# Three value chunks of the spatial gating as blocks in seven products, and its spatial weights loaded at the layer's beginning

## The chip, the core and the metric

The kernel runs on one core of one Trainium2 chip, as one program of some 29,000 instructions. The metric is device time in microseconds (us), the median of several runs.

## The reference, cut to what matters

Two stacks of two layers each work on one sequence of 512 tokens with 1024 features, all in float32. The last layer but the feed-forward is the spatial gating:

```
z = gelu(h @ w_in + b_in)                 # 512x1024 @ 1024x4096
u, v = split(z, 2)                        # 2048 features each
v = layernorm(v, ln_g, ln_b)              # over all 2048 features of a token
sv = einsum('gts,bnsgc->bntgc', ws * tril, v in chunks of 128 tokens) + bs
y = (u * sv) @ w_out                      # 512x2048 @ 2048x1024
```

There are 16 groups g of 128 features; each has its own 128x128 matrix ws over the tokens of a chunk. Ahead of each layer and behind it stand RMS norms whose scales and shifts come from a vector c times `ada_w` (the "ada" sums below).

## The kernel before, in words

Every dense product is made of three matmuls: both operands are split into a high part (float32r, a cast on ScalarE, L191) and a low part (the difference, on VectorE, L192), and `mm3` (L287 to L289) adds high by high, high by low and low by high in one PSUM bank. The layer's input stands transposed in `XH` and `XL` (128 partitions x 8 blocks k of the features x 512 tokens).

`dense` loads a weight in pieces of 256 rows and 512 columns, splits each piece and runs it against four banks. Its tiles are "w" slots of the pool `mid` (4 KB per partition); a new tile takes the slot that has been free for longest, and waits until all its readers are done. The pool `small` (2 KB per partition) has lists "c", "f" and "m" that work alike; `share` moves idle slots between lists.

`seven` computes a product of four blocks by seven block products instead of eight (Winograd's form of Strassen). The token side has `Sums`: four sums of blocks of `XH` and `XL`, each split again. The weight side loads four blocks of 512 rows and 256 columns, makes four differences on GpSimd (L411, L415, L420, L425), splits seven operands, runs seven products of 2 x 4 `mm3` with 256 columns (ring `seven_bank` of six banks) and combines them on ScalarE (L413) and VectorE (L421 to L441); `done` takes each finished block. The feed-forward uses it for six of its eight chunks, in pairs, with the features on the partitions; there `Sums` is made while a dense stage runs, and its fourth sum overwrites a block of `XH` and `XL`.

The spatial gating, `sgu`, makes the 2048 value features in four chunks of 512, with the tokens on the partitions. Chunk 0 (`by_block_first`) goes token block by token block, as the blocks of `XH` are finished. Chunks 1 to 3 go through `dense` with `by_token`. Each bank gets the bias (L1473, VectorE), gelu (L1474, ScalarE) and statistics (L1476, VectorE). Then come mean and variance, and `gate(p)` for p = 0 to 3: normalise the values of chunk p (L1509 to L1511), load 4 groups of spatial weights (`raw`, L1514), transpose them on TensorE (L1517), mask them (L1519), run the dense product of the u half, multiply the values with the spatial weights on TensorE (L1530), add, multiply with u and split. Between gate(2) and gate(3) stands the first half of the output product.

The ada sums are put in between as steps. Each step issues a load of 256 KB and one VectorE operation (L571, L573) into an accumulator; `dense` runs `ada_rate` steps per piece (`ada_go`), and `sgu` has three sums of 20 steps, of which 16 have an operation. What is left is flushed behind gate(3) (`ada_go()`).

All DMAs are issued from SP's queue. The order on each engine is made at build time from the program: among the instructions that the planner holds ready, the one written first goes first; on the chip every engine then keeps that order.

Of the kernel before, what the change touches and what calls it, by code (L numbers as in the profile page):

```python
# [10 lines left out]
F32R = mybir.dt.float32r  # L11
# [19 lines left out]
def kernel(ctx: ExitStack, tc: tile.TileContext, inp: dict, out: bass.AP):  # L31
# [7 lines left out]
    class Ring:  # L39
        def __init__(self, items):  # L40
            self.items, self.i = items, 0
# [78 lines left out]
    def blk(i):  # L120
        return slice(i * P, (i + 1) * P)
# [7 lines left out]
    def by_block(ap):  # L129
        return ap.rearrange("p (c t) -> p c t", t=P)  # L130
# [58 lines left out]
    def split(hi, lo, src):  # L189

        S.copy(hi, src)  # L191
        V.tensor_sub(lo, src, hi.bitcast(F32))  # L192
# [158 lines left out]
    class Sums:  # L351

        def __init__(self):
            def blocks(t):
                return [[t[:, 4 * h : 4 * h + 4, 256 * i : 256 * i + 256] for h in range(2)] for i in range(2)]

            h, l = blocks(XH), blocks(XL)
            hf, lf = ([[b.bitcast(F32) for b in r] for r in m] for m in (h, l))  # L360
            s = [[mid.new("a", [4, 256], F32R) for _ in range(2)] for _ in range(3)]
            s1, s2, s3 = (mid.new("w", [4, 256]) for _ in range(3))
            G.tensor_tensor(s2, lf[1][0], lf[1][1], op=add)
            V.tensor_add(s1, hf[1][0], hf[1][1])
            V.tensor_add(s1, s1, s2)
            split(*s[0], s1)
            G.tensor_tensor(s3, lf[0][0], lf[1][0], op=sub)
            V.tensor_sub(s2, s1, hf[0][0])
            V.tensor_sub(s2, s2, lf[0][0])
            split(*s[1], s2)  # L370
            V.tensor_sub(s1, hf[0][0], hf[1][0])
            V.tensor_add(s3, s3, s1)
            split(*s[2], s3)
            V.tensor_sub(s1, hf[0][1], s2)
            V.tensor_add(s1, s1, lf[0][1])
            split(h[1][0], l[1][0], s1)
            mid.free(s1, s2, s3)
            self.held = [t for p in s for t in p]
            self.of = {"11": (h[0][0], l[0][0]), "12": (h[0][1], l[0][1]), "22": (h[1][1], l[1][1])}
            self.of.update({f"s{i + 1}": s[i] for i in range(3)}, s4=(h[1][0], l[1][0]))  # L380

        def free(self):
            mid.free(*self.held)

    def seven(w, c0, c1, left, done):

# [10 lines left out]
        def product(at, right):  # L399
            b = seven_bank.next()  # L400
            for c in range(2):
                for k in range(4):
                    lh, ll = (t[:, k, blk(c)] for t in right)
                    rh, rl = (t[:, k, :] for t in left.of[at])
                    mm3(b[:, 256 * c : 256 * c + 256], lh, ll, rh, rl, k == 0, k == 3)
            mid.free(*right)
            return b
# [1046 lines left out]
    def sgu(then):  # L1454
# [5 lines left out]
        def row_in(ap):  # L1460
            t = small.new("c", [512])
            nc.sync.dma_start(t, ap.to_broadcast([P, 512]))
            return t
# [25 lines left out]
            return bank  # L1489

        values(0, by_block_first)
        mid.share(w=11, a=16)
        ada_col_steps(1, 3)
        ada_col_steps(1, 4)
        ada_sum(1, 2, lambda: None)
        ada_rate[0] = 2
        for c in range(1, 4):
            values(c, lambda c: dense(w_in, 0, KD, [(2048 + 512 * c, 512)], by_token).__getitem__)
        for tb in range(NB):
            mu, rs = mean_rstd(stats[tb], 1e-6)  # L1500
            V.tensor_copy(v_norm[:, tb, 0:1], rs)
# [2 lines left out]
        def gate(p):  # L1504
# [5 lines left out]
                V.tensor_mul(v, v, gr)  # L1510
                G.tensor_add(v, v, br)  # L1511
            small.free(gr, br)
            raw = row_c.new("c", [512])
            nc.sync.dma_start(by_block(raw), inp["b_ws_2"][0, 4 * p : 4 * p + 4].rearrange("g t s -> t g s"))  # L1514
            b = aux_bank.next()
            for c in range(4):
                T.transpose(b[:, blk(c)], raw[:, blk(c)], ident)  # L1517
# [19 lines left out]
            VV[p].free()  # L1537
            return O

        row_c = small  # L1540
        O = [gate(0), gate(1)]
        Y = [[small.new("f", [512]) for _ in range(2)] for _ in range(NB)]
        of = lambda p, tb: (lambda k: O[p + k // 4](k % 4, blk(tb)))
# [62 lines left out]
```

## Time and profile before

| | us |
|---|---|
| median of 3 runs | 2278.05 (2271.94 to 2279.82) |
| the profiled execution | 2284.42 |
| its span in the trace | 2282.7 |
| TensorE busy | 2226.5 (98%) |
| VectorE busy | 1466.1 (64%) |
| ScalarE busy | 974.4 (43%) |
| GpSimd busy | 236.2 (10%) |

Engines: PE is TensorE, PEld its weight loads, DVE VectorE, ACT ScalarE, POOL GpSimd, SP the queue that issues DMAs. Times in the trace are us from the span's start. A busy TensorE is not TensorE at its peak, since matmuls overlap; distances from start to start tell more. A row of a group reads: line, engine, operation, output <- inputs, shapes, count | busy us, mean ns | idle time ahead of it and what ended it. A wait is put down to the releaser that came last by the profile; where that engine had long been done, it was another, often a DMA.

### The profile page before, as it was taken

The numbers are of one execution on the slowest core, as the hardware profiler recorded it, in microseconds if no ns is written. First come the engines' busy times: TensorE is split into PE (matmuls) and PEld (weight loads), VectorE is DVE, ScalarE is ACT, GpSimd is POOL, SyncE is SP. The second block draws the span as 40 slices with busy tenths as digits, with TensorE's granted clock in tenths as the row PEclk, the third lists the DMA queues.
The fourth block names the chain that finished last, engine by engine and source line by source line (L and its number), as shares of the span: only waits on it lengthen the run. The fifth ranks groups of instructions, "written<-read, shape, count | busy, mean of one in ns | idle before, by whom it ended". The sixth has DMA issues, their size and how long they took to land.

```text
span 2282.7 us, 29350 instructions
## 1 busy us (share of the span) xinstructions
PE 2226.5 (98%) x11112; PEld 1829.6 (80%) x11112; DVE 1466.1 (64%) x2610; ACT 974.4 (43%) x1784; POOL 236.2 (10%) x209
## 2 busy tenths in 40 slices
PE   8999999999999999999999999999999998999998
PEld 6787788787777777887777888988777787898997
DVE  5665755844995857843547847867656747655765
ACT  4333344335344544333444534525524335443543
POOL 0000000100000000100211131221002201031130
PEclk9999999999999999999999999999999999999999
DMA  5343434222222125224413435353254543323322
GB/s 172 111 135 103 146 90 127 93 62 65 85 73 74 38 88 157 79 66 124 144 56 120 156 108 166 103 175 111 74 159 151 157 147 104 108 83 97 116 93 83
DMA packets 158062, 251.16 MB, mean 110 GB/s; under 512 B 13784, under 2 KB 59056, under 8 KB 157920
## 3 DMA queue, kind: packets, MB, share of 16 engines
q1 hardware_dynamic: 157920, 249.29, 34.8%
q8 instruction: 87, 1.43, 0.3%
q14 instruction: 55, 0.45, 0.1%
HBM read 247.15 MB, written 2.10 MB: 109 GB/s over the span
## 4 chain that ended last, share of the span: by engine, by line
PE 77%; DVE 10%; DMA 6%; issue 3%; ACT 3%; POOL 1%; SPq 0%; POOLq 0%; DVEq 0%; ACTq 0%
PE bank L287 23%; PE bank L288 23%; PE bank L289 23%; DMA small<-in_ada_w_dram 3%; DVE mid L192 3%; DVE small L573 2%; PE bank L1109 2%; PE bank L294 1%; DMA mid<-in_ffn_w_dram 1%; ACT mid L191 1%; POOL tiny_c L480 1%; PE bank L1288 1%; PE bank L1293 1%; PE bank L1124 1%; DMA mid<-in_gla_w_in_dram 0%
## 5 line engine op out<-in xcount | busy, mean ns | idle before, releaser
L192 DVE TENSOR_TENSOR mid<-mid,mid 128x512 fp32r<-128x512 f32 (+2 forms) x530 | 512.6, 988 | 457.2 <-ACT mid L191 291.3
L191 ACT CAST mid<-mid 128x512 fp32r<-128x512 f32 (+2 forms) x530 | 419.8, 818 | 769.3 <-DMA mid<-in_ffn_w_dram 139.1
L287 PE MATMUL bank<-mid,mid 128*128 128x512 f32 (+1 forms) x1320 | 491.9, 373 | 5.3 <-DVE small L441 2.7
L288 PE MATMUL bank<-mid,mid 128*128 128x512 f32 (+1 forms) x1320 | 488.3, 370 | 0.0
L289 PE MATMUL bank<-mid,mid 128*128 128x512 f32 (+1 forms) x1320 | 488.1, 370 | 0.0
L287 PE MATMUL bank<-xt_hi,mid 128*128 128x512 f32 (+1 forms) x1216 | 430.2, 355 | 14.7 <-ACT xt_hi L191 9.5
L288 PE MATMUL bank<-xt_lo,mid 128*128 128x512 f32 (+1 forms) x1216 | 428.7, 353 | 3.2 <-DVE xt_lo L192 3.2
L289 PE MATMUL bank<-xt_hi,mid 128*128 128x512 f32 (+1 forms) x1216 | 427.7, 352 | 0.0
L287 PEld LDWEIGHTS bank<-mid,mid 128*128 128x128 f32 x1320 | 248.0, 188 | 53.5 <-DVE small L441 3.5
L289 PEld LDWEIGHTS bank<-mid,mid 128*128 128x128 f32 x1320 | 248.2, 188 | 45.1
L288 PEld LDWEIGHTS bank<-mid,mid 128*128 128x128 f32 x1320 | 248.2, 188 | 43.3 <-issue 0.5
L287 PEld LDWEIGHTS bank<-xt_hi,mid 128*128 128x128 f32 x1216 | 232.5, 192 | 50.9 <-ACT xt_hi L191 11.6
L288 PEld LDWEIGHTS bank<-xt_lo,mid 128*128 128x128 f32 x1216 | 233.2, 192 | 35.6 <-DVE xt_lo L192 4.2
L289 PEld LDWEIGHTS bank<-xt_hi,mid 128*128 128x128 f32 x1216 | 232.8, 191 | 32.1 <-issue 1.3
L287 PE MATMUL bank<-mid,xt_hi 128*128 128x512 f32 (+1 forms) x640 | 252.6, 395 | 0.7 <-ACT mid L191 0.7
L289 PE MATMUL bank<-mid,xt_lo 128*128 128x512 f32 (+1 forms) x640 | 250.4, 391 | 0.8 <-DVE xt_lo L192 0.8
L288 PE MATMUL bank<-mid,xt_hi 128*128 128x512 f32 (+1 forms) x640 | 250.3, 391 | 0.4 <-DVE mid L192 0.4
L573 DVE SCALAR_TENSOR_TENSOR small<-small,c_act,small 128x512 f32<-128x512 f32 x168 | 133.5, 809 | 73.9 <-DMA small<-in_ada_w_dram 72.8
L289 PEld LDWEIGHTS bank<-mid,xt_lo 128*128 128x128 f32 x640 | 120.6, 188 | 28.2 <-DVE xt_lo L192 1.7
L287 PEld LDWEIGHTS bank<-mid,xt_hi 128*128 128x128 f32 x640 | 120.7, 189 | 26.3 <-ACT mid L191 1.2
L288 PEld LDWEIGHTS bank<-mid,xt_hi 128*128 128x128 f32 x640 | 120.6, 188 | 26.2 <-DVE mid L192 0.9
L480 POOL TENSOR_TENSOR tiny_c<-tiny_c,minus_half 128x1 f32<-128x1 f32 (+1 forms) x68 | 53.9, 794 | 722.5 <-DVE tiny_c L494 375.4
(299 smaller groups left out, 2305.4 us busy)
## 6 DMA issues: line engine op xcount, KB each, us to landing
mid<-in_ffn_w_dram SPq DMA_DIRECT2D x128, 512.0 KB, 3.7
small<-in_ada_w_dram SPq DMA_DIRECT2D x192, 256.0 KB, 2.9
mid<-in_dsa_w_in_dram SPq DMA_DIRECT2D x36, 512.0 KB, 3.5
mid<-in_gla_w_in_dram SPq DMA_DIRECT2D x32, 512.0 KB, 4.2
mid<-in_b_w_in_dram SPq DMA_DIRECT2D x32, 512.0 KB, 3.7
mid<-in_a_w_in_dram SPq DMA_DIRECT2D x24, 512.0 KB, 3.9
mid<-in_gla_w_in_dram SPq DMA_DIRECT2D x32, 256.0 KB, 3.0
mid<-in_gla_w_out_dram SPq DMA_DIRECT2D x16, 512.0 KB, 3.7
```

The lines of the kernel that those rows point to most:

```text
L191: S.copy(hi, src)
L192: V.tensor_sub(lo, src, hi.bitcast(F32))
L287: T.matmul(o, lhsT=lh, rhs=rh, start=start, stop=False)
L288: T.matmul(o, lhsT=lh, rhs=rl, start=False, stop=False)
L289: turns.passed(o, T.matmul(o, lhsT=ll, rhs=rh, start=False, stop=stop))
L294: i = T.transpose(b[:, blk(c)], src, ident)
L480: G.tensor_tensor(r, v, minus_half[:, 0:m], op=ALU.pow)
L573: V.scalar_tensor_tensor(a, t, ck, a, op0=mult, op1=add)
L1109: T.matmul(b[:, :n], lhsT=QT[tb][:, blk(c)], rhs=KT[:, :n], start=True, stop=True)
L1124: T.transpose(b[:, blk(c)], es[c][:, blk(j)], ident)
L1288: T.matmul(sb[:, :n], lhsT=KT[pr, c // 2, blk(j)], rhs=QT[pr, c // 2, j * P :], start=True, stop=True)
L1293: T.matmul(nb[i // 2][:, (i % 2) * 129 : (i % 2) * 129 + 129], lhsT=Dm[j][:, blk(i - j)], rhs=vv[j][:, c, :], start=j == 0, stop=j == i)
```

## The change

Chunks 1 to 3 of the values go through `seven` instead of `dense`. For this `Sums(True)` keeps the fourth sum in tiles of its own, since the gates still read `XH` and `XL`, and `seven` gets `by_tokens`: the blocks of tokens become the stationary operand and the blocks of the weight the moving one, so that the tokens stand on the partitions as before. `values_seven` adds the bias to a combined block, applies gelu and takes the statistics once a pair of token blocks is complete. The four loads of spatial weights are issued ahead of the sums into four tiles of list "f", and `gate` takes its own from there. List "c" has 11 tiles instead of 7 during the value chunks. `seven` runs no ada steps.

```diff
-        def __init__(self):
+        def __init__(self, keep=False):
...
-            s = [[mid.new("a", [4, 256], F32R) for _ in range(2)] for _ in range(3)]
+            s = [[mid.new("a", [4, 256], F32R) for _ in range(2)] for _ in range(4 if keep else 3)]
+            s4 = s[3] if keep else (h[1][0], l[1][0])
...
-            split(h[1][0], l[1][0], s1)
+            split(*s4, s1)
...
-            self.of.update({f"s{i + 1}": s[i] for i in range(3)}, s4=(h[1][0], l[1][0]))
+            self.of.update({f"s{i + 1}": s[i] for i in range(3)}, s4=s4)
...
-    def seven(w, c0, c1, left, done):
+    def seven(w, c0, c1, left, done, by_tokens=False):
...
-                    lh, ll = (t[:, k, blk(c)] for t in right)
-                    rh, rl = (t[:, k, :] for t in left.of[at])
+                    still, move = (left.of[at], right) if by_tokens else (right, left.of[at])
+                    lh, ll = (t[:, k, blk(c)] for t in still)
+                    rh, rl = (t[:, k, :] for t in move)
...
         values(0, by_block_first)
+        raws = [small.new("f", [512]) for _ in range(4)]
+        small.share(c=11, f=6)
         mid.share(w=11, a=16)
         ada_col_steps(1, 3)
         ada_col_steps(1, 4)
         ada_sum(1, 2, lambda: None)
         ada_rate[0] = 2
+        for p in range(4):
+            nc.sync.dma_start(by_block(raws[p]), inp["b_ws_2"][0, 4 * p : 4 * p + 4].rearrange("g t s -> t g s"))
+        sums = Sums(True)
+
+        def values_seven(c):
+            VV.append(Quad())
+            br = row_in(inp["b_b_in_2"][:, 2048 + 512 * c : 2560 + 512 * c])
+
+            def done(t, n, b):
+                at = slice(256 * n, 256 * n + 256)
+                b2 = b.rearrange("p (i e) -> p i e", e=256)
+                V.tensor_add(b2, b2, bc(br[:, at], 1, [2, 256]))
+                S.activation(VV[c].ts[t][:, :, at], b2, AF.Gelu)
+                small.free(b)
+                if t != n:
+                    for tb in (2 * t, 2 * t + 1):
+                        V.bn_stats(stats[tb][:, c, :], VV[c][tb])
+
+            c0 = 2048 + 512 * c
+            seven(w_in, c0, c0 + 256, sums, done, True)
+            small.free(br)
+
         for c in range(1, 4):
-            values(c, lambda c: dense(w_in, 0, KD, [(2048 + 512 * c, 512)], by_token).__getitem__)
+            values_seven(c)
...
-            raw = row_c.new("c", [512])
-            nc.sync.dma_start(by_block(raw), inp["b_ws_2"][0, 4 * p : 4 * p + 4].rearrange("g t s -> t g s"))
+            raw = raws[p]
...
-        row_c = small
+        sums.free()
+        small.share(c=7, f=10)
         O = [gate(0), gate(1)]
```

## Rows read from the trace of the kernel before

**Rows 1.** The page's busy times: us, share of the span, instructions of each engine.
```profile
PE 2226.5 (98%) x11112; PEld 1829.6 (80%) x11112; DVE 1466.1 (64%) x2610; ACT 974.4 (43%) x1784; POOL 236.2 (10%) x209
```
**Rows 2.** Stretches of the spatial gating: start:end, length, busy us (instructions) of each engine, granted clock of TensorE, share of the DMA engines, GB/s. Chunks 1 to 3 run from 1637.9, gate(0) to gate(2) from 1705, gate(3) from about 1840.
```profile
1640.00:1660.00 20.00, 20.00 (x88) 16.23 (x87) 8.51 (x10) 6.16 (x8) 0.00 (x0) 1.00 0.34 113
...
1700.00:1720.00 20.00, 16.55 (x68) 13.22 (x67) 15.93 (x32) 10.41 (x15) 6.29 (x10) 0.91 0.57 179
...
1740.00:1760.00 20.00, 17.00 (x74) 13.69 (x73) 14.98 (x24) 4.63 (x6) 5.13 (x4) 0.91 0.48 132
1760.00:1780.00 20.00, 18.49 (x100) 15.47 (x99) 15.17 (x24) 7.02 (x10) 0.00 (x0) 1.00 0.63 184
...
1840.00:1860.00 20.00, 20.00 (x90) 16.28 (x89) 6.64 (x6) 4.87 (x6) 0.00 (x0) 1.00 0.43 135
...
1710.00:1712.00 2.00, 2.00 (x8) 1.61 (x7) 2.00 (x6) 0.00 (x1) 0.00 (x0) 0.50 0.63 173
```
**Rows 3.** TensorE's waits, first two of the spatial gating (1590 to 1900 us), then one of the first feed-forward (1270 to 1560 us): us in total, times, longest.
```profile
PE bank L1517 <- DVE mid L1510: 4.5, 2, 3.0
PE bank L1517 <- DMA small<-in_b_ws_dram: 3.4, 1, 3.4
...
PE bank L287 <- DVE small L433: 1.7, 1, 1.7
```
**Rows 4.** TensorE's timeline at the three groups of transposes: start, us, instruction, and in brackets the idle time before it and what ended it.
```profile
1709.33 1.12 PE L1517 MATMUL bank<-ident,small 128*128 128x128 f32 x4 [3.45 <-DMA small<-in_b_ws_dram]
1710.09 0.78 PE L288 MATMUL bank<-xt_lo,mid 128*128 128x512 f32 x1
...
1712.37 0.45 PE L287 MATMUL bank<-xt_hi,mid 128*128 128x512 f32 x1
...
1746.54 1.02 PE L1517 MATMUL bank<-ident,small 128*128 128x128 f32 x4 [3.00 <-DVE mid L1510]
...
1777.86 0.63 PE L1517 MATMUL bank<-ident,small 128*128 128x128 f32 x4 [1.51 <-DVE mid L1510]
1778.24 0.48 PE L289 MATMUL bank<-xt_hi,mid 128*128 128x512 f32 x1
```
**Rows 5.** DMA issues of two tensors: count, KB each, median us from issue to landing.
```profile
mid<-in_b_w_in_dram SPq DMA_DIRECT2D x32, 512.0 KB, 3.7
...
small<-in_b_ws_dram SPq DMA_DIRECT2D x4, 256.0 KB, 2.8
```
**Rows 6.** Timeline of SP and VectorE around the end of chunk 0, and SP's issue of the spatial weights of gate(1).
```profile
1626.90 0.38 SPq L614 DMA_DIRECT2D small<-in_norm_g_dram  x1
1633.92 4.50 SPq L210 DMA_DIRECT2D mid<-in_b_w_in_dram  x3
...
1630.68 0.69 DVE L192 TENSOR_TENSOR xt_lo<-small,xt_hi 128x512 fp32r<-128x512 f32 x1
...
1638.06 0.69 DVE L1473 TENSOR_TENSOR small<-bank,small 128x512 f32<-128x512 f32 x1 [3.47 <-PE bank L289]
...
1743.60 0.37 SPq L1514 DMA_DIRECT2D small<-in_b_ws_dram  x1
```
**Rows 7.** TensorE's timeline: the first matmul of chunk 1, the last of chunk 3, the first of gate(0).
```profile
1637.86 0.39 PE L287 MATMUL bank<-mid,xt_hi 128*128 128x512 f32 x1
...
1705.26 0.39 PE L289 MATMUL bank<-mid,xt_lo 128*128 128x512 f32 x1
1705.49 0.39 PE L287 MATMUL bank<-xt_hi,mid 128*128 128x512 f32 x1
```
**Rows 8.** A stretch of the first feed-forward in which TensorE runs products of 256 columns alone (columns as in rows 2).
```profile
1355.00:1375.00 20.00, 20.00 (x171) 20.00 (x171) 16.85 (x15) 11.74 (x18) 10.68 (x4) 1.00 0.25 79
```
**Rows 9.** VectorE's timeline in the first feed-forward: two operations of the sums one behind the other, a split beside a GpSimd subtraction, two operations of 512 one behind the other.
```profile
1291.60 1.22 DVE L369 TENSOR_TENSOR mid<-mid,xt_lo 128x1024 f32<-128x1024 f32 x1
1292.73 1.22 DVE L371 TENSOR_TENSOR mid<-xt_hi 128x1024 f32<-128x1024 f32 x1
...
1365.90 2.83 DVE L192 TENSOR_TENSOR mid<-mid,mid 128x1024 fp32r<-128x1024 f32 x1
...
1563.59 0.68 DVE L433 TENSOR_TENSOR small<-small,bank 128x512 f32<-128x512 f32 x1
1564.19 1.22 DVE L192 TENSOR_TENSOR mid<-mid,mid 128x1024 fp32r<-128x1024 f32 x1
```
**Rows 10.** Groups by shape: the first four rows and the last in a pair of `seven` of the feed-forward (1322 to 1382 us, eight GpSimd subtractions), the fifth in the value chunks (1640 to 1682 us, none).
```profile
L192 DVE TENSOR_TENSOR mid<-mid,mid 128x1024 fp32r<-128x1024 f32 x17 | 25.0, 1478 | 26.5 <-PE bank L289 11.2 <-ACT mid L191 11.0 <-PE bank L288 4.2
L192 DVE TENSOR_TENSOR mid<-small,mid 128x512 fp32r<-128x512 f32 x4 | 5.5, 1385 | 0.6 <-ACT mid L191 0.6
L423 DVE TENSOR_TENSOR small<-small,bank 128x512 f32<-128x512 f32 x2 | 1.4, 688 | 0.1
...
L425 POOL TENSOR_TENSOR mid<-mid,mid 128x1024 f32<-128x1024 f32 x2 | 4.8, 2421 | 5.3 <-issue 5.3
...
L192 DVE TENSOR_TENSOR mid<-mid,mid 128x1024 fp32r<-128x1024 f32 x9 | 11.0, 1224 | 19.8 <-ACT mid L191 19.8
...
L191 ACT CAST mid<-mid 128x1024 fp32r<-128x1024 f32 x17 | 17.7, 1050 | 32.5 <-DMA mid<-in_ffn_w_dram 16.1 <-PE bank L288 9.7 <-POOL mid L411 2.5
```
**Rows 11.** Busy time of the ada steps' operation L573 on VectorE in two stretches (count in brackets), granted clock, DMA share, GB/s.
```profile
1640.00:1705.00 65.00, 5.16 (x7) 1.00 0.45 138
...
1800.00:1865.00 65.00, 0.00 (x0) 1.00 0.46 142
```

## The prediction

> **What bounds the kernel now.** I read the page's busy shares first, then TensorE's waits in the stretch of the spatial gating, then the timeline at those waits and at both ends of the value chunks. TensorE is busy for 98% of the span [rows 1], so a change pays by fewer columns on TensorE or by closing its gaps. In the gating layer the gaps are few and sharp: while value chunks 1 to 3 run there is none, in the stretches around 1710, 1750 and 1770 us it loses 3.4, 3.0 and 1.5 us, and in the first two the granted clock falls to 0.91 on the mean [rows 2]. The list of waits puts all three at L1517, the transposes of the spatial weights, one on the DMA of `b_ws`, two on VectorE's L1510 [rows 3]. L1510 has nothing to do with a transpose of `raw`. At the second gap the load was issued at 1743.60, such a load lands after 2.8 us, and the transposes began at 1746.54 [rows 4 to 6]: all three are the same late load, issued only when a "c" tile came free.
>
> **Edit 1: the loads of the spatial weights move to the layer's beginning.** Four issues on SP, 256 KB each, go ahead of the value chunks' loads. SP had nothing to issue from 1626.9 to 1633.92 [rows 6], so they delay nobody. The gain is the three gaps, 3.45 + 3.00 + 1.51 = 8.0 us [rows 4]. After the first two TensorE ran at half speed (granted 0.50, its 1.2 GHz level) for about 3 us: four transposes took 0.76 us where they took 0.38 at the third, and five matmuls 2.28 us where they need 5 x 0.232 [rows 4]. That is 0.4 + 1.1, some 1.6 us each with the second's one more slow matmul, 3.2 in all. What is late next? The first weight pieces of each dense stage had been split before its gap, so I see no second wait behind it. Edit 1: 11.2 us gained. If only the DMA-named wait were a DMA's, it would be 3.45 + 1.6.
>
> **Edit 2, TensorE's part.** Chunks 1 to 3 start on TensorE at 1637.86 and gate(0) at 1705.49 [rows 7]: 67.6 us with 3 x 96 = 288 matmuls of 512 columns, 0.23 us from start to start (66.7 at 0.2315), and some small work that is only moved. After: 3 chunks x 7 products x 2 x 4 x 3 = 504 matmuls of 256 columns. In a stretch of the feed-forward's products 171 of these fill 20 us [rows 8]; from start to start it is 0.1183, so 59.6 us. A chunk needs 19.9 instead of 22.2 us: 7.0 us gained if nothing waits. That is seven eighths by columns, a little worse by the shorter matmul.
>
> **Edit 2, the sums.** `Sums(True)` can begin when the last `xt_lo` is written, 1630.68 + 0.6 = 1631.3, and TensorE has done chunk 0 at 1638.1 [rows 6]. In the feed-forward the same sums lie under a dense stage; here nothing else is ready for TensorE. Product "11" needs no sum, but it needs its weight block loaded, cast (ScalarE) and its low part (VectorE). The "w" tiles that were free early and took the next piece now hold the sums' scratch, so `b11` takes the tile that before got its load at 1633.92: landed at about 1637.6 (3.7 us), cast by 1638.7, and then VectorE [rows 6]. There stand the sums, written earlier in the program, and of ready instructions the order takes the one written first. They are 12 VectorE operations of 128x1024, 1.13 us from start to start [rows 9], 13.6 us, and since one can nearly always run while ScalarE casts for another, I find no hole before the last cast. So the low part of `b11` comes one operation before their end: 1631.3 + 12.5 (eleven of them) + 2.4 (the four 0.6 us operations of chunk 0's last two blocks) + 1.1 (itself) + 2.2 (two GpSimd sums beside it, below) = 1649.5. TensorE waits 11.4 us, and 1.6 us more go to its clock by the price above. Bounds: 1.8 us if it slips in at once (1638.7 + 1.2), without the clock, since the gap of 1.51 us was followed by no slow stretch; 17 us if it comes last and GpSimd stops VectorE for whole instructions three times.
>
> **Edit 2, VectorE in the products.** Per chunk it had four splits and 8 operations of 512, 9.3 us. Now: 7 splits (1.13) and 7 combinations, 4 bias additions and 4 statistics, 15 x 0.60 [rows 9, 10]: 17.0 us against 19.9 of TensorE. On top come four GpSimd subtractions per chunk, 2.4 us or more each [rows 10], which hold VectorE up. How much, c per subtraction, is the open price. From below: in the feed-forward's pair of products the 17 splits of 128x1024 average 1.478 against 1.224 in the value chunks, the 4 of 128x512 1.385 against 0.69: 4.3 + 2.8 us over 8 subtractions, 0.9 [rows 10]. At its busiest, one split took 2.83 for 1.22 [rows 9]. From above: all 2.4. I take 1.1, near the mean, since here VectorE is rarely idle. VectorE then ends its last split, and TensorE its last product, at 1631.3 + 13.6 + 2.4 + 51.0 + 14c - 4.8 (the eight small operations behind the last split) + 2.8 (the product) = 1696.3 + 14c = 1711.7. TensorE by its own columns: 1638.1 + 11.4 + 1.6 + 59.6 = 1710.7. Two bounds so close don't hide in each other: I take 1713 against 1705.5 before, 7.5 us later. Then gate(0) opens on the banks of the last products, its third tile behind the combination L441, 2.8 us after its start; VectorE will be some 4 us behind: 1.5 us (0 to 4). The feed-forward's waits on such combinations show the kind, 1.7 us at L433 [rows 3].
>
> The Trainium skill, "SBUF — State Buffer", section "SBUF: two separate sides", speaks against the change: the port pair shared by VectorE and GpSimd is an exclusive lock for a whole instruction, and the loser fully blocks. The rows agree that both slow each other, but not for whole instructions on the mean. By that rule in full c would be 2.4 and the time that of the third case below; by the rows it is about 1.
>
> **Edit 2, the `ada` steps.** `seven` calls no `ada_go`, so 24 of the 60 steps leave the value chunks in the program, 7 of their operations on VectorE (5.2 us), while none ran between 1800 and 1865 [rows 11]. Late now is the third sum, whose last 12 steps, eight of them with an operation, are flushed behind gate(3). VectorE has 6.6 us of work in 20 there [rows 2], so I cost this at 0; without that cover it is eight times 0.74, 6 us. ScalarE gets 7 casts of 1.05 us per chunk for 4 [rows 10], and is far from full.
>
> **Sum.** +7.5 + 1.5 - 11.2 = -2.2 us against the profiled execution's 2284.4: 2282.2. The same 2.2 off the median of the runs, 2278.05, is 2276.
>
> **The rivals.** (a) *The forecast*: the wait at the first product and VectorE's load eat most of the gain. 0.46. Its own range is 2272 to 2284.
> (b) *Faster*: `b11` slips into an early hole in the sums, and c is 0.8 as over the feed-forward. Then TensorE ends at 1638.1 + 1.8 + 59.6 = 1699.5 and VectorE at 1696.3 + 11.2 = 1707.5; +2.0 + 0.5 - 11.2 = -8.7: 2269. With c near 0.4 it is 2263. It takes an end of the products before 1708.4 to gain 0.3%. For it: VectorE was idle for over 3 us between 1634.5 and 1638.06 before. Against: those holes are now the sums' own. 0.29.
> (c) *Slower*: GpSimd stops VectorE for nearly whole instructions. c = 1.84 moves the end to 1722 and costs 0.3%; c = 2.4 gives 1729.9, +24.4 + 1.5 - 11.2 = +14.7: 2293; half-way, 2287. For it: three chunks without a dense stage between them, where the feed-forward has two, and its pair ends with VectorE behind. Against: the mean of 0.9. 0.20.
> (d) *The early load does not do what it says*: the two waits named L1510 are VectorE's, so 3.00 + 1.51 + 1.6 stay: 2276 + 6 = 2282. Against: issue, landing time and start fit to 0.2 us. 0.05; half of it beyond the bound.
>
> About 0.3%, 6.8 us, is what a measurement of this kernel tells from no change. Faster 0.29; same 0.46 and half of (d), 0.48; slower 0.23. The range runs from (b)'s better end, 2264, to between half and full stop of (c), 2289.
>
> **What would show it.** Right: a TensorE gap of 9 to 13 us between chunk 0 and the first product, ended by VectorE's L192, with the granted clock at half behind it; products over about 60 to 63 us; no wait at L1517; gate(0) from about 1713 to 1715. Wrong if that gap is under 5 us or over 16, if TensorE waits between the products add up to more than 6 us, if the transposes still wait, or if the flushed `ada` steps hold up the last output product at L616.

## The result, and the profile after

The changed kernel took 2304.85 us (median), the kernel before 2277.24 beside it: a ratio of 1.0118, 95% interval 1.007 to 1.0166. It is slower by some 28 us, beyond the upper end of the prediction's range (2289). The profiled executions are 2302.6 us of span after and 2282.7 before.

The page's busy times of the kernel after, to be read beside [rows 1]:

```profile
PE 2225.2 (97%) x11328; PEld 1838.6 (80%) x11328; DVE 1530.1 (66%) x2652; ACT 989.0 (43%) x1800; POOL 277.7 (12%) x223
```

TensorE's busy time hardly fell, although its columns did: matmuls at half speed count as busy. VectorE has 64 us more. To see where the 20 us of span are I cut both traces at four matmuls: the first of chunk 0, the first of gate(0), the end of the last values by spatial weights, and the first of 256 columns in the feed-forward behind. These are the stages of both, and of the experiments told below (us):

| kernel | up to chunk 0 | values | gates | output product | rest | span |
|---|---|---|---|---|---|---|
| before | 1610.6 | 94.9 | 162.3 | 54.1 | 360.9 | 2282.7 |
| after | 1607.0 | 119.9 | 156.7 | 55.8 | 363.3 | 2302.6 |
| e1, early loads alone | 1601.9 | 96.1 | 159.3 | 54.2 | 361.6 | 2273.0 |
| e2, seven products alone | 1611.4 | 120.3 | 164.5 | 56.3 | 362.8 | 2315.2 |
| e3, differences on VectorE | 1610.1 | 112.6 | 159.6 | 55.6 | 362.8 | 2300.8 |
| e4, no differences | 1605.6 | 100.7 | 159.7 | 57.5 | 362.7 | 2286.1 |
| e5, chunk 1 dense | 1616.8 | 104.8 | 161.6 | 53.5 | 361.9 | 2298.6 |
| e7, more weight tiles | 1608.8 | 115.2 | 157.5 | 55.8 | 362.3 | 2299.7 |
| e8, transposes early | 1614.2 | 96.6 | 164.7 | 53.4 | 361.8 | 2290.8 |
| e9, ada steps between | 1621.4 | 125.3 | 164.7 | 53.6 | 361.6 | 2326.6 |
| e10, e5 without differences | 1605.3 | 97.0 | 157.9 | 53.7 | 362.1 | 2275.9 |
| e12, transposes a gate ahead | 1607.7 | 95.2 | 165.8 | 53.2 | 360.6 | 2282.4 |
| e13, three ada steps | 1602.5 | 96.1 | 159.0 | 54.8 | 360.7 | 2273.1 |

The first column is work that no kernel here changes, and it varies by up to 19.5 us from one execution to the next; so one profile's span says little, and the stages are compared instead. Each row is one execution; where two kernels run nearly the same code, a stage agrees to about 1 us (values of 94.9, 96.1 and 96.1 with dense chunks, of 119.9 and 120.3 by seven). From before to after: values +25.0, gates -5.6, behind them +4.1, upstream -3.6 by chance; together +19.9.

TensorE's timeline after, at the waits of the value stage (columns as in [rows 4]):

```profile
1644.74 0.58 PE L287 MATMUL bank<-mid,xt_hi 128*128 128x256 f32 x1 [10.36 <-ACT mid L191]
...
1645.69 0.58 PE L287 MATMUL bank<-mid,mid 128*128 128x256 f32 x1 [0.37 <-ACT mid L191]
...
1647.93 0.58 PE L288 MATMUL bank<-mid,xt_hi 128*128 128x256 f32 x1 [1.66 <-DVE mid L192]
...
1654.06 0.39 PE L287 MATMUL bank<-mid,xt_hi 128*128 128x256 f32 x1 [1.51 <-ACT mid L191]
...
1680.31 0.39 PE L288 MATMUL bank<-mid,mid 128*128 128x256 f32 x1 [3.03 <-DVE mid L192]
...
1687.18 0.39 PE L288 MATMUL bank<-mid,xt_hi 128*128 128x256 f32 x1 [0.85 <-DVE mid L192]
...
1700.86 0.38 PE L288 MATMUL bank<-mid,xt_hi 128*128 128x256 f32 x1 [2.05 <-DVE mid L192]
...
1706.99 0.58 PE L288 MATMUL bank<-mid,mid 128*128 128x256 f32 x1 [3.04 <-DVE mid L192]
```

The stretches of that stage (columns as in [rows 2]):

```profile
1640.00:1660.00 20.00, 11.51 (x57) 10.31 (x57) 19.96 (x14) 8.94 (x10) 7.53 (x3) 0.63 0.04 13
1660.00:1680.00 20.00, 16.82 (x136) 16.29 (x136) 17.18 (x15) 7.05 (x9) 8.37 (x3) 1.00 0.31 106
1680.00:1700.00 20.00, 17.65 (x144) 17.21 (x144) 18.44 (x21) 7.57 (x10) 5.32 (x3) 1.00 0.33 107
1700.00:1720.00 20.00, 16.10 (x112) 15.89 (x113) 20.00 (x17) 7.58 (x9) 8.48 (x3) 0.83 0.12 32
```

Where the kernel before had TensorE full and VectorE at 8 of 20 us, VectorE is now busy for 17 to 20 of 20 us, and TensorE waits for its splits and runs at half speed (granted 0.50, 1.2 GHz) behind some of the waits: 64 starts of matmuls come 0.2 us or more apart where they need 0.118, which adds up to 6.5 us. All waits from the one ahead of the first product to gate(0) are 23.5 us. With the chunks' 59.4 us at full speed (504 by 0.1178) these are 89.4 of the 92.5 us between chunk 0's last matmul and gate(0).

The waits at the transposes of the spatial weights, [rows 3], are gone. In the gates TensorE's list of waits now reads (1726 to 1880 us):

```profile
PE bank L287 <- ACT small L1575: 2.6, 1, 2.6
PE bank L289 <- DVE mid L192: 1.9, 1, 1.9
```

### The profile page after: what moved, and what is told of

It reads as the page before. It is cut to its first block, busy times and chain, and to the rows that moved or that the text cites. A ratio compares the mean times of both kernels' runs of the same rounds, so it can differ in the third digit from the quotient of the medians.

```text
span 2302.6 us, 29877 instructions
## 1 busy us (share of the span) xinstructions
PE 2225.2 (97%) x11328; PEld 1838.6 (80%) x11328; DVE 1530.1 (66%) x2652; ACT 989.0 (43%) x1800; POOL 277.7 (12%) x223
## 4 chain that ended last, share of the span: by engine, by line
PE 76%; DVE 11%; DMA 5%; issue 3%; ACT 3%; POOL 2%; SPq 0%; DVEq 0%; POOLq 0%; ACTq 0%
PE bank L287 22%; PE bank L288 22%; PE bank L289 22%; DVE mid L192 4%; DMA small<-in_ada_w_dram 3%; PE bank L1112 2%; DVE small L576 1%; PE bank L294 1%; ACT mid L191 1%; POOL tiny_c L483 1%; PE bank L1291 1%; PE bank L1296 1%; DMA mid<-in_ffn_w_dram 1%; PE bank L1127 1%; PE bank L1556 1%
## 5 line engine op out<-in xcount | busy, mean ns | idle before, releaser
L192 DVE TENSOR_TENSOR mid<-mid,mid 128x512 fp32r<-128x512 f32 (+2 forms) x543 | 545.7, 1026 | 415.4 <-ACT mid L191 238.7
L191 ACT CAST mid<-mid 128x512 fp32r<-128x512 f32 (+2 forms) x543 | 433.2, 824 | 756.8 <-PE bank L288 140.0
L287 PE MATMUL bank<-mid,mid 128*128 128x512 f32 (+1 forms) x1416 | 522.0, 369 | 10.9 <-DVE small L444 3.1
L288 PE MATMUL bank<-mid,mid 128*128 128x512 f32 (+1 forms) x1416 | 518.6, 366 | 6.7 <-DVE mid L192 6.7
L289 PE MATMUL bank<-mid,mid 128*128 128x512 f32 (+1 forms) x1416 | 517.7, 366 | 0.0
L287 PEld LDWEIGHTS bank<-mid,mid 128*128 128x128 f32 x1416 | 268.8, 190 | 60.1 <-DVE small L444 4.0
L288 PEld LDWEIGHTS bank<-mid,mid 128*128 128x128 f32 x1416 | 268.5, 190 | 51.0 <-DVE mid L192 7.5
L289 PEld LDWEIGHTS bank<-mid,mid 128*128 128x128 f32 x1416 | 269.0, 190 | 45.2
L287 PEld LDWEIGHTS bank<-xt_hi,mid 128*128 128x128 f32 x1216 | 230.5, 190 | 49.0 <-ACT xt_hi L191 11.2
L287 PE MATMUL bank<-mid,xt_hi 128*128 128x512 f32 (+2 forms) x616 | 235.9, 384 | 12.6 <-ACT mid L191 12.6
L288 PE MATMUL bank<-mid,xt_hi 128*128 128x512 f32 (+2 forms) x616 | 233.8, 379 | 5.1 <-DVE mid L192 5.0
L289 PE MATMUL bank<-mid,xt_lo 128*128 128x512 f32 (+2 forms) x616 | 233.6, 379 | 0.8 <-DVE xt_lo L192 0.8
L576 DVE SCALAR_TENSOR_TENSOR small<-small,c_act,small 128x512 f32<-128x512 f32 x168 | 133.0, 806 | 73.5 <-DMA small<-in_ada_w_dram 72.9
L287 PEld LDWEIGHTS bank<-mid,xt_hi 128*128 128x128 f32 x616 | 117.0, 190 | 34.6 <-ACT mid L191 13.7
L288 PEld LDWEIGHTS bank<-mid,xt_hi 128*128 128x128 f32 x616 | 116.9, 190 | 27.7 <-DVE mid L192 6.4
```

Source lines behind the costliest of these rows:

```text
L287: T.matmul(o, lhsT=lh, rhs=rh, start=start, stop=False)
L288: T.matmul(o, lhsT=lh, rhs=rl, start=False, stop=False)
L289: turns.passed(o, T.matmul(o, lhsT=ll, rhs=rh, start=False, stop=stop))
L576: V.scalar_tensor_tensor(a, t, ck, a, op0=mult, op1=add)
```

## The experiments

My first theory after the result: GpSimd's differences stop VectorE, in each chunk anew, and that costs more than the sums. Rivals: the sums at the start, which nothing covers; too few weight tiles; the early loads; the moved ada steps. Each kernel is compared with runs of the kernel before beside it.

### e1: the early loads alone

```
+        raws = [small.new("f", [512]) for _ in range(4)]
+        small.share(c=11, f=6)
...
+        for p in range(4):
+            nc.sync.dma_start(by_block(raws[p]), inp["b_ws_2"]...)
...
-            raw = row_c.new("c", [512])
-            nc.sync.dma_start(by_block(raw), inp["b_ws_2"]...)
+            raw = raws[p]
```

> Edit 1 alone: the four loads of spatial weights ahead of the value chunks, chunks 1 to 3 in dense as before. Theory A (the three gaps at L1517 were late loads, and nothing else stands behind them): the gaps go and with them the half-speed stretches, 8.0 + 3.2 us, about 2267 against 2277. Rival (other waits take their place, as in the changed kernel, whose time from gate(0) to the end of gate(3) fell by 5.3 us only): 2272. If the two waits named L1510 were VectorE's, they stay: 2273.

Measured: 2275.52 us, ratio 0.9984 (0.9967 to 1.0002). TensorE's waits between 1690 and 1860 us, to be read beside the first two of [rows 3]:

```profile
PE bank L1520 <- DVE small L1535: 4.2, 2, 4.0
PE bank L287 <- DVE v_norm L1505: 1.4, 1, 1.4
```

No wait names the DMA any more, but 5.6 us of the 8.0 us of waits are back. VectorE, ScalarE and TensorE at the longest one:

```profile
1726.71 1.04 ACT L191 CAST mid<-mid 128x1024 fp32r<-128x1024 f32 x1 [1.97 <-DMA mid<-in_b_w_in_dram]
...
1727.79 1.23 DVE L192 TENSOR_TENSOR mid<-mid,mid 128x1024 fp32r<-128x1024 f32 x1 [4.12 <-ACT mid L191]
...
1728.93 0.69 DVE L1535 TENSOR_TENSOR small<-bank,small 128x512 f32<-128x512 f32 x1
...
1729.67 1.12 PE L1520 MATMUL bank<-ident,small 128*128 128x128 f32 x4 [4.00 <-DVE small L1535]
```

L1535 is gate(0)'s bias addition, which reads a bank of the ring from which the transposes of gate(1) take theirs. It stands on VectorE behind a split, the split behind a cast, and the cast behind a late load of `w_in`. Behind this wait TensorE ran at half speed again (granted 0.50 until 1735.5). So a second wait stood behind the load of the spatial weights, as the rival said. Edit 1 is worth some 3 us of stage, not 11.2, and the medians with their interval don't tell it from nothing.

### e2: the seven products alone

```
-        raws = [small.new("f", [512]) for _ in range(4)]
...
-            raw = raws[p]
+            raw = small.new("c", [512])
+            nc.sync.dma_start(by_block(raw), inp["b_ws_2"]...)
```

> Edit 2 alone: chunks 1 to 3 by seven products, the spatial weights loaded inside the gates as before. Theory A (edit 1 is worth the same with either kind of chunk): 2305 + 5 to 11, so 2310 to 2316. Rival (behind the products VectorE and not the load is late, so edit 1 was worth little there): within 3 us of the changed kernel's 2305.

Measured: 2309.38 us, ratio 1.0132 (1.0107 to 1.0156). The values take 120.3 us, as in the full change: the whole loss is the seven products', and the early loads have no part in it. The gates are 7.8 us longer than in the full change, though the transposes wait for the DMA only 0.82 us here; 0.86 us more stand at a gelu, 1.45 at a combination as gate(0) opens, the wait at a copy of the output product is 4.75 us instead of 2.58, and half speed follows it (granted 0.50 until 1851.47, some 2.1 us lost): 0.82 + 0.86 + 1.45 + 2.2 + 2.1 = 7.4. That is one execution, 7.6 us above the median of its kernel. By the ratios (1.0132 against 1.0118) the early loads are worth some 3 us beside the seven products, within the intervals, and as much as alone; that they are worth more there is not shown.

### e3: the same four differences, on VectorE

```
-        G.tensor_tensor(b12, b12, b11, op=sub)
+        V.tensor_sub(b12, b12, b11)        # in the gating; the other three alike
```

> The changed kernel with the four differences of weight blocks per chunk on VectorE instead of GpSimd, in the spatial gating alone. Theory A (each GpSimd difference stretches one VectorE operation by some 2 us where VectorE has no idle time): VectorE per chunk 17.0 + 4 x 1.13 = 21.5 us instead of about 26.6, so products 1 to 3 get some 15 us shorter, and the first wait 2 us: about 2288. Rival (the pace is set by the order of the products on TensorE or by late weight blocks, not by the stretched operations): 2300 or more, and the pattern of 3.0 us waits stays.

Measured: 2300.49 us, ratio 1.0081 (1.0057 to 1.0105). VectorE's groups by shape from 1630 to 1725 us, first of the changed kernel:

```profile
L192 DVE TENSOR_TENSOR mid<-mid,mid 128x1024 fp32r<-128x1024 f32 x26 | 49.0, 1892 | 2.9 <-ACT mid L191 2.9
L1513 DVE TENSOR_TENSOR small<-small,small 128x512 f32<-128x512 f32 x9 | 10.6, 1176 | 0.2
...
L370 DVE TENSOR_TENSOR mid<-mid,xt_lo 128x1024 f32<-128x1024 f32 x1 | 3.4, 3355 | 0.0
```

and then of e3:

```profile
L192 DVE TENSOR_TENSOR mid<-mid,mid 128x1024 fp32r<-128x1024 f32 x27 | 32.7, 1220 | 6.1 <-ACT mid L191 5.4 <-PE bank L289 0.7
L1525 DVE TENSOR_TENSOR small<-small,small 128x512 f32<-128x512 f32 x11 | 7.6, 687 | 0.1
...
L415 DVE TENSOR_TENSOR mid<-mid,mid 128x1024 f32<-128x1024 f32 x3 | 3.7, 1222 | 1.8 <-DMA mid<-in_b_w_in_dram 1.8
```

The same splits average 1.892 us beside GpSimd and 1.220 without. 26 x 0.672 + 9 x 0.489 + 2.13 (L370) = 24.0 us of VectorE's time, over twelve differences 2.0 us each. On VectorE itself a difference costs 1.22. So GpSimd took nothing off VectorE; it cost it more than doing the work. Against the theory: the values became shorter by 7.3 us only, where some 17 were expected, and the time is the one that the rival named (2300 or more), though the pattern of 3.0 us waits that the rival wanted is gone. The differences are now links of a chain: load, difference, cast, split. TensorE's waits from the first product to gate(0) in e3:

```profile
PE bank L287 <- ACT mid L191: 12.0, 6, 6.0
PE bank L288 <- DVE mid L192: 4.7, 4, 2.6
```

They fell from 23.5 to 16.7 us, but a good part now ends with a cast. So the stop is a part of the loss and not all of it.

### e4: no differences at all

```
-        G.tensor_tensor(b12, b12, b11, op=sub)
+        pass                               # in the gating; t2 is a copy of b22 on ScalarE
```

> The changed kernel with the four differences of weight blocks per chunk left out in the spatial gating (one becomes a copy on ScalarE, the others nothing), so the value chunks 1 to 3 are not the reference's. Theory A: VectorE needs 17.0 us per chunk, less than TensorE's 19.9, so the products run at TensorE's pace, about 60 us for three chunks behind a first wait of 8 us with its slow clock: some 22 to 25 us less than the changed kernel, 2281. Rival (order or loads set the pace): 2297 or more.

Measured: 2286.06 us, ratio 1.0034 (1.0015 to 1.0053). The values take 100.7 us, 19.2 less than after. Two stretches of it:

```profile
1660.00:1680.00 20.00, 20.00 (x171) 20.00 (x171) 17.65 (x23) 10.87 (x14) 0.00 (x0) 1.00 0.40 131
1680.00:1700.00 20.00, 20.00 (x171) 20.00 (x171) 17.32 (x22) 10.43 (x13) 0.00 (x0) 1.00 0.39 108
```

Here 171 matmuls fill 20 us, the rate of [rows 8] on which the prediction rested: with VectorE at 17.5 of 20 the products do keep TensorE full. What is left over the kernel before is 5.8 us: waits at the start (9.7 us in all) and slow matmuls (2.4), less the 7 us of fewer columns. So the differences are worth 19 us, and the entry with the open sums some 12. How much of the 19 is the stop of VectorE and how much the longer chain of load, difference, cast and split is not separated: e3 took away the stop alone and gave 7.3.

### e5 and e10: the sums covered, with and without the differences

```
+        values(1, lambda c: dense(w_in, 0, KD, [(2048 + 512 * c, 512)], by_token).__getitem__)
         sums = Sums(True)
...
-        for c in range(1, 4):
+        for c in range(2, 4):
             values_seven(c)
```

> Chunk 1 stays dense, as before; the sums are made under it, and only chunks 2 and 3 go by seven, with GpSimd's differences. Theory A (two costs: the sums lie open before the first product, some 11 to 17 us with the half clock behind; and VectorE's load in each chunk by seven, about 26 us for 19.9 us of TensorE): the gap ahead of the first product goes, and each chunk by seven still costs some 4 us more than dense, so the values take 95 + 8 = 103 us from chunk 0's first matmul to gate(0), and the kernel is 10 to 17 us below the changed one: 2288 to 2295. Theory B (the sums alone are the cost, and the chunks by seven follow on at TensorE's rate when they don't start behind): values 90 to 93 us, kernel 2275 to 2279.

Measured: 2293.58 us, ratio 1.0043 (1.0018 to 1.0068); values 104.8 us against 103 by theory A. The gap ahead of the first product did not go altogether, as theory A had it: 4.7 us are left. With the sums under a dense chunk the kernel is still slower than before, by 10 us of the value stage for two chunks. Theory B is out.

e10 is e5 with the edit of e4 on top.

> Both suspected costs taken away together: chunk 1 stays dense with the sums made under it, and chunks 2 and 3 go by seven without their four differences (left out, so four of seven products of each have other numbers in them). If the sums lying open and the differences are the whole loss: the values take the 104.8 us of the version with chunk 1 dense less 2 x 6.4 (a third of what leaving out the differences of three chunks gave, each) = 92 us, 3 us below the 94.9 of the kernel before and near the 90.2 that two chunks' fewer columns allow; the kernel is 0 to 6 us below the one before. If something third is lost (the banks, the combinations, the entry into gate(0)): values 96 us or more.

Measured: 2280.82 us, ratio 0.9993 (0.9975 to 1.001); values 97.0 us. That is a miss: 92 was expected if sums and differences were the whole loss. TensorE's waits from 1650 to 1703 us:

```profile
PE bank L287 <- ACT mid L191: 2.8, 2, 1.8
PE bank L288 <- DVE mid L192: 0.7, 1, 0.7
```

All of it is the entry into the first chunk by seven, 3.9 us with 1.8 us of half speed behind: ScalarE is busy 4.00 of 4.00 us from 1660 to 1664, where the gelu of the dense chunk and the casts for the first products meet, and VectorE too. From the first product on, 336 matmuls take 46.1 us where 39.6 would do. A part of the crowd is the experiment's own, the copy that stands in for a difference:

```profile
1658.87 1.03 ACT L422 COPY mid<-mid 128x1024 f32<-128x1024 f32 x1
...
1660.86 1.03 ACT L191 CAST mid<-mid 128x1024 fp32r<-128x1024 f32 x1
```

TensorE's longest wait, 1.8 us, ends with this cast, and the copy stands ahead of it in ScalarE's order. So there is a third cost, a crowded entry, of some 5 to 6 us, and with it two chunks by seven win nothing even with the differences left out and the sums covered.

### e7: more tiles for weight blocks

```
-        mid.share(w=11, a=16)
+        mid.share(w=15, a=12)              # 13 and 14 from chunk 2, 11 and 16 from chunk 3
```

> The changed kernel, with 15 tiles for weight blocks (and 12 of the other kind) in chunk 1, 13 and 14 in chunk 2, 11 and 16 in chunk 3, where it has 11 and 16 throughout; so the first blocks of chunk 1 can be loaded while the sums hold their scratch. Theory A (VectorE's and GpSimd's work sets the pace, the order of VectorE's instructions puts the sums first): within 4 us of the changed kernel, values 116 to 121 us. Rival (the first block's late tile and load set the first wait): the gap of 10.4 us before the first product goes to 5 us or less, values 112 or less, the kernel 8 us or more below the changed one.

Measured: 2301.69 us, ratio 1.0091 (1.0058 to 1.0125); values 115.2 us, 4.7 less than after, between the two. TensorE's first waits:

```profile
1643.97 0.58 PE L287 MATMUL bank<-mid,xt_hi 128*128 128x256 f32 x1 [5.52 <-ACT mid L191]
...
1649.78 0.58 PE L288 MATMUL bank<-mid,xt_hi 128*128 128x256 f32 x1 [4.07 <-DVE mid L192]
...
1658.73 0.58 PE L287 MATMUL bank<-mid,mid 128*128 128x256 f32 x1 [3.68 <-ACT mid L191]
```

The earlier tile halves the first wait, as the rival says, and two others grow behind it: 13.3 us in three, where the changed kernel has 14.5 in six. All waits of the stage fall from 23.5 to 18.0 us. So the late tile was worth some 5 us, and the rest stays without it. The kernel's time is theory A's (3.2 us below the changed kernel), its 116 us for the values are just missed, and none of the rival's marks was reached.

### e9: ada steps between the chunks

```
         def values_seven(c):
...
+            ada_go(8)
             seven(w_in, c0, c0 + 256, sums, done, True)
```

> The changed kernel, with eight steps of the ada sums written ahead of each chunk by seven, as the dense chunks had them among their products; so fewer are left for the later stages. The part from the last output product's end to the end of the kernel, and the output product, were 2.4 and 1.7 us longer in the changed kernel than before. If the moved ada steps are why: both go back, 4 us in all, and the values take 0 to 8 us more, since seven of VectorE's operations of 0.74 us go into stretches in which it is full. If they are not: the tail stays at +4 us.

Measured: 2317.87 us, ratio 1.0157 (1.0119 to 1.0194). The output product went back by 2.1 us and the rest behind it by 1.7: 3.8 of the 4.1 us, so the moved ada steps are what lengthened the tail. It fits the other kernels: the output product takes 55.6 us or more in those that run no ada step among their value chunks, and 53.2 to 54.8 in those that do. How they did it is seen in the changed kernel:

```profile
1881.48 0.75 DVE L576 SCALAR_TENSOR_TENSOR small<-small,c_act,small 128x512 f32<-128x512 f32 x1 [2.28 <-DMA small<-in_ada_w_dram]
...
1884.02 1.12 PE L619 MATMUL bank<-small,ones 128*128 128x512 f32 x2 [0.47 <-DVE small L1558]
```

A flushed ada step (L576) waits for its load, VectorE's L1558 stands behind it and a split, and TensorE waits for L1558 at L619, the line that the prediction calls L616; in the kernel before there is no such wait. But the values took 5.4 us more, since VectorE has no room for the steps, and the gates 8.1, which was not foreseen: 9.4 us of waits where the changed kernel has 4.5, and two stretches at half speed (granted clock 0.91 and 0.83 on the mean of 20 us). So moving these steps out of the chunks was no loss on the whole, but it was not free.

### e8, e12 and e13: is there more in the early loads?

e8 and e12 are e1 with the transposes and the mask moved, into the loaded tile; in e8 all four to the layer's beginning, in e12 those of the next gate ahead of a gate's own products:

```
+        for p in range(4):                 # e8, behind the early loads
+            b = aux_bank.next()
+            for c in range(4):
+                T.transpose(b[:, blk(c)], raws[p][:, blk(c)], ident)
+            V.tensor_mul(by_block(raws[p]), by_block(b), bc(tri, 1, [4, P]))
```

> The early loads alone (chunks all dense), with the transposes and masks of the four spatial weights moved to the layer's beginning too, into the loaded tiles. Theory (the loads alone gained 3 us in the gates, because the transposes then waited for the bank that the gate before still read): the waits at the transposes go altogether, the gates take 154 to 156 us where the kernel before took 162.3, the values 96 us, and the kernel is 6 to 9 us below the one before, 2268 to 2271. Rival (TensorE's waits move on to the v_norm at L1505 and to the eviction of the last gate's products): gates 158 or more, the kernel within 4 us of the one before.

Measured: 2286.56 us, ratio 1.0014 (0.9995 to 1.0032); gates 164.7 us: the rival. The waits at the transposes are gone, and these stand in their place (1690 to 1860 us, the longer group):

```profile
PE bank L287 <- ACT small L1529: 10.4, 3, 5.3
```

L1529 is the gelu that empties the banks of a gate's own product. ScalarE at the longest of the three, and SP ahead of it:

```profile
1759.00 4.66 SPq L562 DMA_DIRECT2D small<-in_ada_w_dram  x4
...
1763.75 0.38 SPq L210 DMA_DIRECT2D mid<-in_b_w_in_dram  x1
...
1768.62 1.05 ACT L191 CAST mid<-mid 128x1024 fp32r<-128x1024 f32 x1 [5.31 <-DMA mid<-in_b_w_in_dram]
...
1776.21 0.69 ACT L1529 ACTIVATE small<-bank,vec 128x512 f32<-128x512 f32 x1 [0.58 <-DVE mid L192]
```

A load of `w_in` is issued behind four ada loads, its cast stands ahead of the gelu in ScalarE's order, and TensorE waits for the gelu's bank.

> The early loads alone (chunks all dense), with the transposes and the mask of the next gate's spatial weights written ahead of a gate's own products, into the loaded tile, where the early loads alone had them at the next gate's beginning, behind the four banks of the products. Theory (the early loads alone left 5.6 us of waits at the transposes, 4.0 of them for a bank that the gate before still read): no wait at the transposes, gates 155 to 158 us, kernel 5 to 8 us below the one before. Rival (the stage is short of weight tiles and of VectorE's and ScalarE's turns, and a wait taken away comes back elsewhere, as it did with all transposes at the layer's beginning): gates 159 to 165 us, the kernel within 3 us of the one with the early loads alone.

Measured: 2282.22 us, ratio 1.0006 (0.9988 to 1.0023); gates 165.8 us: no gain, as the rival says, and a little beyond it, since the ratio is some 5 us above e1's where it said 3 (1.0006 against 0.9984, the intervals overlap). TensorE now waits at the products, for the mask's multiplication (L1512), which reads the bank they want:

```profile
1731.87 1.04 ACT L191 CAST mid<-mid 128x1024 fp32r<-128x1024 f32 x1 [2.25 <-DMA mid<-in_b_w_in_dram]
...
1732.95 1.23 DVE L192 TENSOR_TENSOR mid<-mid,mid 128x1024 fp32r<-128x1024 f32 x1 [4.46 <-ACT mid L191]
...
1734.09 0.68 DVE L1512 TENSOR_TENSOR small<-bank,tri 128x512 f32<-128x512 f32 x1
...
1734.83 1.44 PE L1537 MATMUL bank<-small,mid 128*128 128x128 f32 x5 [5.34 <-DVE small L1512]
```

e13 is e1 with three ada steps to a block:

```
-        ada_rate[0] = 2
+        ada_rate[0] = 3
```

> The early loads alone (chunks all dense), with three steps of the ada sums to a block where there were two, so that the sums' loads and VectorE's operations end earlier, inside the dense value chunks, where VectorE has 8 of 20 us of work. If the ada loads on SP and VectorE's operations in the gates are what the weights of the gates wait for: gates 156 or less, kernel 3 to 6 us below the early loads alone. If not: within 3 us of it.

Measured: 2281.05 us, ratio 0.9993 (0.9975 to 1.0011); gates 159.0 us against e1's 159.3. So the ada steps as such are not what the gates wait for. In e1 and e12 the chain is the same: a late load, a cast, a split, and behind the split on VectorE the operation that would set a bank free. Whoever needs that bank next waits. What makes the load late, the weight tiles or their order on SP, was not separated. No version here is measurably faster than the kernel before; e1 comes nearest.

## Why the prediction was wrong, point by point

**What bounds the kernel.** Right for before. Not seen: VectorE takes over as the bound in the value stage; the prediction had both bounds within 1 us of each other and should have priced what happens when VectorE's is the higher one.

**c, the price of a difference: the step that failed.** Taken 1.1, measured 2.0 (24.0 us over twelve). VectorE and GpSimd in chunk 3 of the changed kernel:

```profile
1697.34 2.39 POOL L414 TENSOR_TENSOR mid<-mid,mid 128x1024 f32<-128x1024 f32 x1 [11.29 <-DMA mid<-in_b_w_in_dram]
...
1698.34 2.47 DVE L192 TENSOR_TENSOR mid<-mid,mid 128x1024 fp32r<-128x1024 f32 x1 [1.46 <-ACT mid L191]
...
1699.81 3.26 POOL L418 TENSOR_TENSOR mid<-mid,mid 128x1024 f32<-128x1024 f32 x1
...
1700.73 2.88 DVE L1513 TENSOR_TENSOR small<-small,small 128x512 f32<-128x512 f32 x1
...
1703.14 2.71 POOL L423 TENSOR_TENSOR mid<-mid,mid 128x1024 f32<-128x1024 f32 x1
...
1703.54 3.40 DVE L192 TENSOR_TENSOR mid<-mid,mid 128x1024 fp32r<-128x1024 f32 x1
...
1709.99 2.70 POOL L428 TENSOR_TENSOR mid<-mid,mid 128x1024 f32<-128x1024 f32 x1 [4.14 <-issue]
...
1710.38 3.39 DVE L192 TENSOR_TENSOR mid<-mid,mid 128x1024 fp32r<-128x1024 f32 x1
```

Take the ends. GpSimd's end at 1699.73, 1703.07, 1705.85 and 1712.69; the VectorE operation beside each ends at 1700.81, 1703.61, 1706.94 and 1713.77: 1.08, 0.54, 1.09 and 1.08 us later. That is the time of a whole split (1.13 from start to start), and of a whole small operation (0.60), after GpSimd is done. From the moment such an operation stood beside the difference, VectorE got nothing done until the difference had ended. All twelve differences of the stage show it. The operations that were stopped had both inputs in SBUF; one that reads a PSUM bank was not, here in chunk 2:

```profile
1670.65 2.39 POOL L414 TENSOR_TENSOR mid<-mid,mid 128x1024 f32<-128x1024 f32 x1 [12.67 <-DMA mid<-in_b_w_in_dram]
...
1671.19 0.69 DVE L440 TENSOR_TENSOR small<-small,bank 128x512 f32<-128x512 f32 x1 [0.72 <-PE bank L289]
```

The mean of 0.9 that I took from the feed-forward [rows 10] was no milder stop: there six of VectorE's operations ended 1.08 or 0.55 us after GpSimd, two of the eight subtractions met VectorE idle (26.5 us of idle time ahead of its splits), and combinations that read a bank ran on beside others in 0.68 us. The change also adds to what can be stopped: its bias addition (L1513) reads the combined block from SBUF, where the dense chunks' L1473 reads a bank; 4.4 of the 24.0 us fell on these additions. A mean over a stretch with idle time priced a stretch without any. The row that belonged to it was the split of 2.83 us [rows 9]. This is what the Trainium skill says, "SBUF — State Buffer", section "SBUF: two separate sides": the port pair that VectorE and GpSimd share is an exclusive lock, and the loser fully blocks. The prediction quoted it and set the mean against it; these rows agree with the page.

**What c makes of the sum.** In the prediction's formula VectorE's bound is 1696.3 + 14 x 2.0 = 1724.3, 11.3 us above the 1713 taken. With that alone the sum is +18.8 + 1.5 - 11.2 = +9.1, 2287 us: rival (c), whose mechanism held. (Its "half-way, 2287" is not half-way by its own formula, which gives 2284 for c midway between 1.1 and 2.4; 2287 belongs to c = 2.0.) The stages add 4.7 us in the values (25.0 against 18.8 + 1.5), 5.6 less gained in the gates and 4.1 behind them: +23.5. The medians are 27.6 apart; the 4 us left are less than the part up to chunk 0 varies. The 11.3 is the formula's and not an experiment's: with the differences on VectorE, at 1.13 for 2.0, the formula gains some 10 us, and e3 gained 7.3.

**Half speed.** Taken 1.6 us for one gap; measured 6.5, since there are three slow stretches (0.63 on the mean from 1640 to 1660, 0.83 from 1700 to 1720). The last of them helped to put TensorE behind VectorE: VectorE's last split of the stage ended at 1719.56 and TensorE's last product at 1726.55, 7.0 us later where 2.8 was taken, +4.2, of which this slow stretch is some 2.6 by my estimate (5.8 us with a start every 0.213 us for 0.118). With 11.3 that is 15.5 of the 16.0 us by which the value stage missed (+25.0 against +9.0).

**The first wait.** Size right: 10.4 us, 11.4 predicted (and 4.1 in five pieces behind it). The mechanism was half right, so the size is partly luck: it ended with a cast, not with the split. The cast of `b11` stood on ScalarE behind that of a sum, which waited 7.24 us for VectorE's L370, and that and a split ahead of it were stopped by two differences of chunk 1 that ran during the sums already. The prediction had put only GpSimd's two sums there.

**Columns.** Right: 0.1178 us a matmul, 59.4 us for 59.6; e4 shows the rate without a wait.

**Edit 1.** The load was what the transposes waited for [rows 3, 4], and the issue was early enough. "I see no second wait behind it" failed: 8.0 us of waits became 5.6 in e1, and the gates gained 3.0 us there and 5.6 in the changed kernel, for 11.2 predicted.

**The ada steps and the tail.** Taken at 0, because VectorE would have room for them; that failed too. Behind the gates the changed kernel has 4.1 us more, and e9 brought back 3.8 of it. The 6 us that the prediction gave for the case without that room were nearer.

**What would show it.** The text named over 6 us of waits between the products as a sign that it was wrong. They are 9.0 us from 1680 on, at four places. It also named flushed `ada` steps that hold up the last output product; that came as well, with 0.7 us at L619.

## What to carry to other kernels

Before work is moved from VectorE to GpSimd, look at whether VectorE is idle in that very stretch: where it was full, and worked on operations with both inputs in SBUF, a GpSimd operation of two tensors took 2.0 us from VectorE on the mean, for work that VectorE did itself in 1.22. A saving of columns on TensorE is worth what the slowest of its suppliers lets through, so make VectorE's sum for the stage with stretched operations and compare the two before counting columns. And ahead of a removed wait, follow the bank, not only the operand: what would the instruction wait for next?

## What the runs showed of the hardware

A VectorE operation with both inputs in SBUF that meets a running GpSimd subtraction of 128x1024 ends one full duration of its own (1.08 or 0.54 us) after GpSimd, in all twelve cases of the value stage. One that reads a PSUM bank is not held up: 0.68 and 0.69 us beside a running GpSimd (L1476 at 1630.25, L440 at 1671.19). GpSimd pays as well: the same subtraction took 2.39 us where it started beside an idle VectorE or such an operation, and up to 3.26 otherwise, ending 2.2 to 2.3 us after the VectorE operation it had met. Half speed was dearer than the 1.6 us a gap taken from before: behind the wait of 3.04 us at 1706.99 the granted clock stayed at 0.50 until past 1712, and behind waits of 3.03 and 2.05 us at 1680.31 and 1700.86 it stayed at 1.00.
